# Attention norms of a hybrid decoder trunk: one product with ones from folded squares

## The chip, the core and the metric

The kernel runs on one core of a Trainium2 chip. The metric is device time in microseconds (us) of one launch. Its engines work side by side, each from its own queue in order: PE (TensorE, matrix products, with weight loads listed as PEld), DVE (VectorE), ACT (ScalarE), POOL (GpSimd) and SP (SyncE, which here only issues transfers). Engines wait for each other by semaphores. An instruction that waits holds up everything behind it in the same queue.

## The reference, cut to what matters

One decoder layer over 1024 positions and 1024 channels. The input is normalised, one wide product gives queries, keys, values and gates of two head groups, each group's output is normalised per head and gated, and a last product mixes them:

```python
h = rms_norm(x, pre_g)
z = jnp.einsum('bsd,de->bse', h, w_in)
qa, ka, va, ga, qb, kb, vb, gb, gk_low = split_columns(z)
...
oa = diff_attention(...)                                  # 8 heads, 128 value channels each
oa = rms_norm(oa, subln_g) * (1.0 - lam_init)             # mean square over the 128 channels of a head
oa = oa.reshape(B, S, DA_WIDTH) * jax.nn.silu(ga)
...
ob = rms_norm(gla_chunked(...), gla_g)                    # 4 heads, 256 channels each
y = jnp.einsum('bse,ed->bsd', jnp.concatenate([oa, ob], axis=-1), w_out)
return x + rms_norm(y, post_g)
```

The change is in the second line of the middle part: the mean square of each attention head over its 128 channels.

## The kernel before, in words

All products run on PE in a reduced-precision type (fp32r). To keep float32 accuracy an operand is split in two parts: ACT copies it to fp32r (the high part), DVE subtracts that copy from the original (the low part), and PE multiplies the parts one after the other into the same accumulator.

The kernel has three stages. Up to about 650 us it makes the wide input product and, woven into it, the gated linear attention. From there to about 965 us it runs the softmax attention together with a large part of the output product. Then it ends with the last quarter of the output product and the last norm.

In the attention stage `merge` weaves three streams together by a cost that each step yields: `all_scores` (line 1065; scores, mask and minimum on DVE, exponential on ACT, combination of the two maps on POOL and DVE at lines 1053 and 1056), `all_values` (line 1171; transposes of the weights on PE, their split into `wt_hi` on ACT at line 1096 and `wt_lo` on DVE at line 1097, products `po` with the values) and `out_early` (line 1238; products `ypart`, later `yps`, of the output product). The position of every PE instruction is fixed by this weave (`mm` and `tr`, lines 116 and 119, keep program order). The order on ACT, DVE and SP is not: there the library's scheduler places every instruction that isn't pinned, by a plan of its own made when the kernel is built. So an edit can change the order of instructions on ACT and DVE that it doesn't touch.

`attn_norm(h, half, o)` (line 1128) runs 16 times, for 8 heads and two halves of 512 positions. Its operand `o` holds one head's 128 value channels in 128 rows and 512 positions in columns. It works like this:

- ACT squares `o` into `sq` (line 1135), ACT makes the high part of `sq` in `hl[:, 0]` (line 1137), DVE the low part in `hl[:, 1]` (line 1138).
- After two steps of the weave that give other streams' work to PE, PE multiplies both parts with a 128 x 128 matrix of ones (`ms`, lines 1142 to 1144): the sum over the 128 rows, the same in every row.
- ACT makes the inverse root (lines 1148 and 1149), DVE scales `o` (line 1150), POOL multiplies by the gate (line 1151), SP stores the result to memory (`mixd`, line 1153). For the last head the result stays on chip, and `last_part` (line 1215) splits it for the output product: ACT makes `m_hi` at line 1218, DVE `m_lo` at line 1219.

`early_ends` (line 1324) is what PE does between the last head's two norms: it starts with the half that was normalised first, so PE's products `yps` there need `m_hi` and `m_lo` of that half while the other half's norm is being made.

Of the kernel before, what the change touches and what calls it, by code (L numbers as in the profile page):

```python
# [8 lines left out]
F32 = mybir.dt.float32  # L9
F32R = mybir.dt.float32r  # L10
AF = mybir.ActivationFunctionType
ALU = mybir.AluOpType
PSUM = bass.MemoryType.PSUM

P = 128
# [16 lines left out]
def hymba_kernel(  # L32
# [21 lines left out]
    act, dve, pool, pe, sp = nc.scalar, nc.vector, nc.gpsimd, nc.tensor, nc.sync  # L54

    def fp(t):
        return t.bitcast(F32)

    def cols(half):
        return slice(half * 512, half * 512 + 512)  # L60
# [8 lines left out]
    ones = const.tile([P, P], F32R, name="ones")  # L69
# [34 lines left out]
    def bank(i, shape, name):  # L104
        return psum.tile(shape, F32, tag=f"b{i}", name=name)
# [10 lines left out]
    def mm(*a, **k):  # L116
        tc.keep_in_program_order(pe.matmul(*a, **k))  # L117
# [99 lines left out]
    i = order.index((1, 4))  # L217
# [520 lines left out]
    decay(3)  # L738


    def mean_square(os, tile):

        sq = tile("sq")
        act.activation(sq, os[0], AF.Square)
        for o in os[1:]:
            sq2 = tile("sq")
            act.activation(sq2, o, AF.Square)
            dve.tensor_tensor(sq, sq, sq2, ALU.add)
        return sq
# [18 lines left out]
    def gla(g):  # L768

        u = None  # L770
        for half in range(2):
# [46 lines left out]
            for m in range(2):  # L818
# [14 lines left out]
                yield  # L833
            gla_loads(*((g, 1) if half == 0 else (g + 1, 0)))
            sq = mean_square([o[:, 0], o[:, 1]], t_c)
            hl = kp.tile([P, 2, 512], F32R, tag="k1", name="sq_hl")
            act.copy(hl[:, 0], sq)
# [133 lines left out]
    smp = smp_cm.__enter__()  # L971
# [156 lines left out]
    def attn_norm(h, half, o):  # L1128
        if h < DA_HEADS - 1:
            gate = smp.tile([P, 512], F32, tag="gate", name="gate", bufs=2)  # L1130
        else:
            gate = kp.tile([P, 512], F32, tag=("q1", "k1")[half], name="gate")
        sp.dma_start(gate, g_d[h][:, cols(half)])
        sq = smp.tile([P, 512], F32, tag="r", name="sq", bufs=1)
        act.activation(sq, o, AF.Square)
        hl = smp.tile([P, 2, 512], F32R, tag="sq_hl", name="sq_hl", bufs=1)
        act.copy(hl[:, 0], sq)
        dve.tensor_tensor(hl[:, 1], sq, fp(hl[:, 0]), ALU.subtract)
        yield 0.0
        yield 0.0  # L1140
        n_tr[0] += 1
        ms = bank(TR[n_tr[0] % 2], [P, 512], "ms")
        for i in range(2):
            mm(ms, ones, hl[:, i], start=(i == 0), stop=(i == 1))
        if h == DA_HEADS - 1 and not half:
            opened[TR[n_tr[0] % 2]] = None
        r = smp.tile([P, 512], F32, tag="r", name="r", bufs=1)
        act.activation(r, ms, AF.Ln, bias=eps_t, scale=1.0 / P)
        act.activation(r, r, AF.Exp, scale=-0.5)
        dve.scalar_tensor_tensor(r, o, sub_g, r, ALU.mult, ALU.mult)  # L1150
        pool.tensor_tensor(gate, r, gate, ALU.mult)
        if h < DA_HEADS - 1:
            sp.dma_start(mixd[h * P : (h + 1) * P, cols(half)], gate)
            stored.append(h)
        else:
            last_mix[half] = gate
        yield 0.0
# [13 lines left out]
    def all_values():  # L1171
        carry = iter(())
        nxt = v_first
        for h in range(DA_HEADS):
            v = nxt
            o = [smp.tile([P, 512], F32, tag="o", name="o", bufs=3) for _ in range(2)]
            yield from mingle(values(h, 3, v, o[1]), carry)
            if h + 1 < DA_HEADS:
                nxt = load_v(h + 1)
            yield from values(h, 2, v, o[1])  # L1180
            yield from mingle(
                chain(values(h, 1, v, o[0]), values(h, 0, v, o[0])), attn_norm(h, 1, o[1])
            )
            carry = attn_norm(h, 0, o[0])
        yield next(carry)
        yield lambda: (ENDS[2], 0) in ps_d
        early_ends()
        yield from carry
# [313 lines left out]
```

## Time and profile before

| | |
|---|---|
| median of 3 runs | 1001.05 us (999.26 to 1002.24) |
| the profiled execution's own time | 1001.76 us |
| its span, first to last instruction | 1000.1 us |
| `ms` products | 32, first at 685.3 us, last at 961.3 us |
| `attn_norm` calls | 16 |

The profile gives for each engine its busy time, for groups of instructions their mean time and what ended the idle time ahead of them, and a chain of waits followed back from the last instruction. Times in it are microseconds from the span's start unless marked ns. In a timeline row the first number is the start, the second the duration, and a remark in brackets is idle time of that engine just before, with what ended it. A row of matmuls with "x2" merges two. A PE duration runs from the start to the modelled end of a pipelined product, so the distance between two starts, not the duration, says what a product costs PE.

### The profile page before, as it was taken

The numbers are of one execution on the slowest core, as the hardware profiler recorded it, in microseconds if no ns is written. First come the engines' busy times: TensorE is split into PE (matmuls) and PEld (weight loads), VectorE is DVE, ScalarE is ACT, GpSimd is POOL, SyncE is SP. The second block draws the span as 40 slices with busy tenths as digits, with TensorE's granted clock in tenths as the row PEclk, the third lists the DMA queues.
The fourth block names the chain that finished last, engine by engine and source line by source line (L and its number), as shares of the span: only waits on it lengthen the run. The fifth ranks groups of instructions, "written<-read, shape, count | busy, mean of one in ns | idle before, by whom it ended". The sixth has DMA issues, their size and how long they took to land.

```text
span 1000.1 us, 16216 instructions
## 1 busy us (share of the span) xinstructions
PE 971.5 (97%) x5546; PEld 845.6 (85%) x5546; DVE 726.2 (73%) x1434; ACT 595.5 (60%) x1164; POOL 135.6 (14%) x145
## 2 busy tenths in 40 slices
PE   6999999999999999999999999999999999999997
PEld 5998988888889997998888888788888888888775
DVE  6886697789767487566777675577777787877646
ACT  7642464586465455445557665367666667777764
POOL 5200000000000000000200000022221232343232
PEclk9999999999999999999999999999999999999999
DMA  9443366746766678886978867996565679974658
GB/s 354 130 120 101 112 165 213 236 154 230 257 222 191 212 242 259 262 248 212 288 230 270 263 211 260 317 349 198 182 222 192 198 273 365 293 187 80 171 178 171
DMA packets 152595, 220.48 MB, mean 220 GB/s; under 512 B 17104, under 2 KB 83664, under 8 KB 152416
## 3 DMA queue, kind: packets, MB, share of 16 engines
q1 hardware_dynamic: 148480, 212.10, 65.3%
q0 software_dynamic: 4032, 7.34, 4.8%
q8 instruction: 44, 0.72, 0.3%
q14 instruction: 39, 0.32, 0.1%
HBM read 133.93 MB, written 88.60 MB: 223 GB/s over the span
## 4 chain that ended last, share of the span: by engine, by line
PE 83%; DMA 5%; DVE 4%; ACT 3%; issue 2%; POOL 1%; SPq 0%; DVEq 0%; POOLq 0%; ACTq 0%
PE x L117 21%; PE y L117 14%; PE z L117 14%; PE ypart L117 11%; PE sc L117 6%; PE po L117 4%; PE yps L117 3%; PE gpo L117 2%; PE wtr L120 2%; DMA v_d<-v_st 1%; PE kv L117 1%; DMA wo_raw<-in_w_out_dram 1%; DVE p L1037 1%; PE gkl_ps L117 1%; POOL p L1053 1%
## 5 line engine op out<-in xcount | busy, mean ns | idle before, releaser
L315 ACT CAST w<-w_raw 128x512 fp32r<-128x512 f32 (+1 forms) x164 | 112.7, 688 | 95.0 <-PE y L117 48.5
L316 DVE TENSOR_TENSOR w<-w_raw,w 128x512 fp32r<-128x512 f32 (+1 forms) x164 | 127.0, 776 | 56.3 <-ACT w L315 46.8
L1047 ACT ACTIVATE p<-p,stt 128x896 f32<-128x896 f32 (+7 forms) x128 | 99.5, 778 | 46.7 <-DVE stt L1037 45.5
L428 ACT COPY s<-x 128x512 f32<-128x512 f32 x84 | 49.0, 583 | 102.0 <-PE x L117 101.8
L1037 DVE CUSTOM_DVE_ANT_0 p<-sc,maskt 128x512 f32<-128x512 f32 (+3 forms) x128 | 74.8, 586 | 26.1 <-PE sc L117 25.0
L1053 POOL TENSOR_SCALAR p<-p,stt,lam 128x1024 f32<-128x1024 f32 (+3 forms) x64 | 54.9, 863 | 252.6 <-DVE stt L1052 252.3
L296 DVE TENSOR_TENSOR w_raw<-w_raw 128x512 f32<-128x512 f32 (+1 forms) x96 | 75.4, 786 | 16.2 <-DMA w_raw<-in_w_in_dram 15.0
L117 PE MATMUL y<-h_hi,w 128*128 128x512 f32 x320 | 81.2, 396 | 0.0
L117 PE MATMUL z<-s_hi,w 128*128 128x512 f32 x320 | 80.2, 393 | 0.0
L785 POOL TENSOR_SCALAR_AFFINE_SELECT gan<-gan 128x512 f32<-128x512 f32 x8 | 13.0, 1631 | 494.0 <-ACT gan L784 494.0
L117 PE MATMUL x<-s_hi,w 128*128 128x512 f32 x320 | 80.0, 392 | 0.0
L117 PE MATMUL ypart<-wo_hi,m_hi 128*128 128x512 f32 x192 | 79.5, 414 | 0.1
L117 PE MATMUL ypart<-wo_hi,m_lo 128*128 128x512 f32 x192 | 75.6, 394 | 0.0
L117 PE MATMUL ypart<-wo_lo,m_hi 128*128 128x512 f32 x192 | 75.4, 393 | 0.0
L117 PE MATMUL sc<-k,q 128*128 128x512 f32 (+1 forms) x192 | 70.7, 371 | 2.1 <-DVE stt L1037 2.1
L117 PEld LDWEIGHTS y<-h_hi,w 128*128 128x128 f32 x320 | 60.2, 191 | 12.1
L117 PEld LDWEIGHTS x<-s_hi,w 128*128 128x128 f32 x320 | 59.4, 188 | 11.9
L117 PEld LDWEIGHTS z<-s_hi,w 128*128 128x128 f32 x320 | 59.2, 188 | 11.7
L117 PE MATMUL sc<-ks,q 128*128 128x512 f32 (+1 forms) x192 | 66.6, 349 | 0.0
L1056 DVE SCALAR_TENSOR_TENSOR p<-p,stt,p 128x1024 f32<-128x1024 f32 (+3 forms) x64 | 52.6, 824 | 15.1 <-POOL p L1053 14.5
L117 PEld LDWEIGHTS po<-wt_hi,v 128*128 128x128 f32 x320 | 54.1, 188 | 7.1 <-ACT wt_hi L1096 0.8
L117 PE MATMUL po<-wt_hi,v 128*128 128x256 f32 (+1 forms) x320 | 58.9, 275 | 0.6 <-ACT wt_hi L1096 0.6
(220 smaller groups left out, 2273.6 us busy)
## 6 DMA issues: line engine op xcount, KB each, us to landing
w_raw<-in_w_in_dram SPq DMA_DIRECT2D x56, 512.0 KB, 4.6
wo_raw<-in_w_out_dram SPq DMA_DIRECT2D x32, 256.0 KB, 3.4
k_d<-qk_st SPq DMA_DIRECT2D x64, 128.0 KB, 2.5
q_d<-qk_st SPq DMA_DIRECT2D x64, 128.0 KB, 3.6
wo_d<-wo_hi SPq DMA_DIRECT2D x32, 256.0 KB, 2.6
wo_d<-wo_raw SPq DMA_DIRECT2D x32, 256.0 KB, 3.2
v_d<-v_st SPq DMA_DIRECT2D x64, 128.0 KB, 3.6
q<-q_d SPq DMA_DIRECT2D x32, 256.0 KB, 5.4
```

The lines of the kernel that those rows point to most:

```text
L117: tc.keep_in_program_order(pe.matmul(*a, **k))
L120: tc.keep_in_program_order(pe.transpose(dst, src, ident))
L296: dve.tensor_tensor(dst, a, b, ALU.subtract)
L315: act.copy(w[0], src)
L316: dve.tensor_tensor(w[1], src, fp(w[0]), ALU.subtract)
L428: act.copy(b[k], ps)
L785: pool.affine_select(a, a, [[0, 4], [1, P]], ALU.is_ge, 0.0, base=0, channel_multiplier=-1)
L1037: ins = dve.tensor_tensor_reduce(p[:, a:e], sc[:, : e - a], maskt[:, NZ + P - (e - a) :] if last else maskt[:, : e - a], 1.0, 3e38 if i == ...
L1047: act.activation(p[:, :n], p[:, :n], AF.Exp, bias=st[:, m : m + 1], scale=-1.0, accum_out=st[:, 2 + m : 3 + m],)
L1053: pool.tensor_scalar(p1[:, :n], p1[:, :n], st[:, 5:6], lam, ALU.mult, ALU.mult)
L1056: dve.scalar_tensor_tensor(p0[:, :n], p0[:, :n], st[:, 4:5], p1[:, :n], ALU.mult, ALU.subtract)
```

## The change

```diff
+    def both_parts(dst, src):
+
+        act.copy(dst[:64], src[:64])
+        dve.tensor_tensor(dst[64:], src[:64], fp(dst[:64]), ALU.subtract)
...
         sq = smp.tile([P, 512], F32, tag="r", name="sq", bufs=1)
-        act.activation(sq, o, AF.Square)
         hl = smp.tile([P, 2, 512], F32R, tag="sq_hl", name="sq_hl", bufs=1)
-        act.copy(hl[:, 0], sq)
-        dve.tensor_tensor(hl[:, 1], sq, fp(hl[:, 0]), ALU.subtract)
+        fold = smp.tile([P, 512], F32, tag="fold", name="fold", bufs=1)
+        act.activation(fold[:64], o[64:], AF.Square)
+        act.activation(sq[:64], o[:64], AF.Square)
+        dve.tensor_tensor(sq[:64], sq[:64], fold[:64], ALU.add)
+        both_parts(hl[:, 0], sq)
         yield 0.0
         yield 0.0
         n_tr[0] += 1
         ms = bank(TR[n_tr[0] % 2], [P, 512], "ms")
-        for i in range(2):
-            mm(ms, ones, hl[:, i], start=(i == 0), stop=(i == 1))
+        mm(ms, ones, hl[:, 0], start=True, stop=True)
```

Rows 64 to 127 of `o` are squared into rows 0 to 63 of a new tile, rows 0 to 63 into `sq`, and DVE adds the two. The sum has 64 rows. Its high part goes to rows 0 to 63 of `hl[:, 0]`, its low part to rows 64 to 127, so that one product with ones sums both. A norm then has two squares and a copy on ACT (before: one and a copy), an addition and a subtraction on DVE (before: a subtraction), all on 64 rows of 512, and one product on PE (before: two). The new tile takes 2 KB a row of its own; no other tile gets another place.

On PE the two programs have the same order but for the 16 products that are gone. On DVE and ACT the scheduler also places other instructions differently around the norms. The DVE orders at the places that the text below speaks of, with `p 512` for the minimum of line 1037 at 512 columns, `recip` for line 1052 and `p896` for line 1056 at 896 columns:

```
first norm of the first head:
  before  recip, p 512, p896, p 256, r, p 512, wt_lo
  after   p 512, recip, p 256, p896, r, p 512, wt_lo
  (the fifth head's first norm had this second order before, too)
second norm of the third head:
  before  p 512, wt_lo, p768, sq_hl, p 128, wt_lo, p 512
  after   p 512, sq, p768, wt_lo, p 128, wt_lo, sq_hl
second norm of the fourth head:
  before  wt_lo, p 512, p768, sq_hl, p 128, wt_lo, p 512
  after   p 512, sq, p768, wt_lo, p 128, wt_lo, sq_hl
second norm of the seventh head:
  before  p 512, p768, wt_lo, sq_hl, p 128, m_lo, wt_lo, m_lo
  after   p 512, sq, p768, wt_lo, p 128, m_lo, wt_lo, sq_hl, m_lo
last norm of all:
  before  sq_hl, m_lo x4
  after   sq, sq_hl, m_lo x4
```

On SP a store or a load of two heads stands one to three transfers earlier or later; POOL's order is the same.

## The prediction

> **What bounds the kernel now.** I read the page first: busy time, granted clock and the engines' shares of the chain of waits.
>
> ```profile
> PE 971.5 (97%) x5546; PEld 845.6 (85%) x5546; DVE 726.2 (73%) x1434; ACT 595.5 (60%) x1164; POOL 135.6 (14%) x145
> PEclk9999999999999999999999999999999999999999
> PE 83%; DMA 5%; DVE 4%; ACT 3%; issue 2%; POOL 1%; SPq 0%; DVEq 0%; POOLq 0%; ACTq 0%
> ```
>
> PE is busy almost throughout at its full granted clock, and 83% of the chain is PE's own work. A pipelined engine can look busier than it is, so the second view is the busy time by stretch: attention up to where its last norms begin, and the 25 us that hold those two.
>
> ```profile
> 665.00:940.00 275.00, 273.57 (x1592) 237.30 (x1591) 209.72 (x576) 195.28 (x436) 81.81 (x89) 1.00 0.72 220
> 940.00:965.00 25.00, 23.19 (x119) 18.23 (x118) 7.22 (x18) 12.85 (x30) 1.94 (x3) 1.00 0.47 159
> ```
>
> The columns are PE, PEld, DVE, ACT and POOL. Up to 940 us PE has no idle time to speak of (1.4 of 275 us), but DVE is at 76% and ACT at 71%; after that PE has gaps. So the first stretch is PE's with two engines close behind, and the second is a chain between PE, ACT and DVE. The third view is what PE's weight loads wait for in the attention stage, longest first:
>
> ```profile
> PEld po L117 <- DVE wt_lo L1097: 3.1, 9, 0.9
> ```
>
> Nine times PE already stands still because DVE's low part of the transposed weights (`wt_lo`) comes too late. DVE's reserve there is a matter of tenths of a microsecond, and the change puts work on DVE.
>
> **What is removed.** 16 products with ones go. What one costs PE is the distance between starts, not its duration of 394 ns:
>
> ```profile
> 685.33 0.62 PE L117 MATMUL ms<-sq_hl,ones 128*128 128x512 f32 x2
> 685.79 0.39 PE L117 MATMUL po<-wt_hi,v 128*128 128x256 f32 x2
> ```
>
> Two take 0.46 us (685.33 to 685.79), so one takes 0.23 us. The last norm of all gives nothing: behind its products PE waits for `m_hi` of the other half, which ACT makes behind a copy that has nothing to do with this norm:
>
> ```profile
> 961.57 0.39 PE L117 MATMUL yps<-wo_hi,ones 128*128 128x512 f32 x1
> 962.18 0.50 PE L117 MATMUL yps<-wo_hi,m_hi 128*128 128x512 f32 x1 [0.22 <-ACT m_hi L1218]
> ```
>
> The product behind `ms` starts at 961.57 and is issued by 961.80; the next one starts at 962.18, so 0.38 us are lost there already, and 0.23 us more or less ahead of them change nothing. That leaves 15 x 0.23 = 3.5 us saved.
>
> **What is added.** ACT gets one more square, DVE one more addition per norm, all on 64 rows. The trace has no 64-row instruction, but it has both ends:
>
> ```profile
> L1135 ACT ACTIVATE sq<-o x16: 631/633/634, 678.8 to 955.9; 128x512 f32<-128x512 f32 x16
> L1138 DVE TENSOR_TENSOR sq_hl<-sq,sq_hl x16: 680/688/694, 681.3 to 957.3; 128x512 fp32r<-128x512 f32 x16
> L748 DVE TENSOR_TENSOR sq<-sq x8: 684/690/693, 300.8 to 569.6; 128x512 f32<-128x512 f32 x8
> L676 DVE TENSOR_TENSOR gkl<-low,gkl x2: 680/680/681, 84.0 to 90.6; 16x512 fp32r<-16x512 f32 x2
> ```
>
> The same subtraction takes 680 ns on 16 rows, the addition 690 ns on 128: the number of rows doesn't matter, so 64 rows are as dear as 128. I take 0.63 us for the square and 0.69 us for the addition. Back to back they cost their queues about 0.53 and 0.61 us (below, 770.63 to 771.24 for a DVE instruction of this size). The way from `o` to the product grows by both: 0.64 + 0.02 + 0.69 + 0.02 = 1.37 us. For most norms two steps of the weave lie in between and cover it: the first norm's low part starts at 681.3 and is ready at 682.0, 3.3 us ahead of its product at 685.33. The copy on ACT now waits for DVE's addition, where before it followed ACT's own square; behind it stand `wt_hi` and exponentials, for which `wt_lo`, `po` and the scores' combination wait. In most norms the scheduler has put the copy one to three instructions further back, so that the addition is done by then. The delay shows where DVE's queue had no reserve, or where nothing lies in between. I went through the places where the two programs' DVE orders differ.
>
> *The last norm of all* (second half of the last head). This piece of the chain of waits is made of the norm's own steps:
>
> ```profile
> 955.95 0.64 ACT sq L1135
> 956.61 0.63 ACT sq_hl L1137
> 957.26 0.22 DVE sq_hl L1138
> 957.87 0.30 DVE m_lo L1219
> 958.22 3.07 PE yps L117 x12
> ```
>
> PE's `yps` products wait for `m_lo` of the other half. `m_lo` and the `m_hi` that it needs stand behind this norm's subtraction on DVE and its copy on ACT, and keep that place. Both start 1.37 us later, `m_lo` too, and PE has nothing else in front: +1.4 us, not covered.
>
> *The first head's first norm.* The combination `p896` now stands behind the next scores' `p 256`, and `recip`, which feeds POOL's half of it, behind `p 512`. The trace has a case of that order, at the fifth head:
>
> ```profile
> 840.17 0.48 DVE L1037 CUSTOM_DVE_ANT_0 p<-sc,maskt,stt 128x256 f32<-128x256 f32 x1 [1.30 <-PE sc L117]
> 840.58 1.15 DVE L1056 SCALAR_TENSOR_TENSOR p<-p,stt,p 128x896 f32<-128x896 f32 x1
> 842.38 0.40 PE L117 MATMUL po<-wt_hi,v 128*128 128x256 f32 x2
> 843.52 0.39 PE L117 MATMUL po<-wt_lo,v 128*128 128x256 f32 x1 [0.75 <-DVE wt_lo L1097]
> ```
>
> DVE stands idle until the scores come, everything behind is late, and PE loses 1.14 - 0.24 = 0.9 us (0.24 is the undisturbed distance, 771.87 to 772.11 below). At the first head the old order kept `wt_lo` ready 0.15 us ahead of its use:
>
> ```profile
> 689.36 0.56 DVE L1097 TENSOR_TENSOR wt_lo<-wtr,wt_hi 128x384 fp32r<-128x384 f32 x1
> 690.07 0.29 PE L117 MATMUL po<-wt_lo,v 128*128 128x256 f32 x1
> ```
>
> With the fifth head's order: +0.9 us.
>
> *Second norms of the third, fourth and seventh heads.* There `wt_lo` moves behind the addition and, in the first two, behind `p768` (0.92 us from start to start):
>
> ```profile
> 770.63 0.69 DVE L1097 TENSOR_TENSOR wt_lo<-wtr,wt_hi 128x512 fp32r<-128x512 f32 x1
> 771.24 1.01 DVE L1056 SCALAR_TENSOR_TENSOR p<-p,stt,p 128x768 f32<-128x768 f32 x1
> 772.16 0.68 DVE L1138 TENSOR_TENSOR sq_hl<-sq,sq_hl 128x512 fp32r<-128x512 f32 x1
> 771.87 0.40 PE L117 MATMUL po<-wt_hi,v 128*128 128x256 f32 x2
> 772.11 0.28 PE L117 MATMUL po<-wt_lo,v 128*128 128x256 f32 x1
> ...
> 808.05 0.69 DVE L1097 TENSOR_TENSOR wt_lo<-wtr,wt_hi 128x512 fp32r<-128x512 f32 x1
> 810.25 0.28 PE L117 MATMUL po<-wt_lo,v 128*128 128x256 f32 x1
> ...
> 925.38 0.68 DVE L1097 TENSOR_TENSOR wt_lo<-wtr,wt_hi 128x512 fp32r<-128x512 f32 x1
> 926.12 0.38 PE L117 MATMUL po<-wt_lo,v 128*128 128x256 f32 x1
> ```
>
> Third head: 0.61 + 0.92 = 1.53 us later against a reserve of 772.11 - 771.32 = 0.79: +0.7. Fourth: `p 512` comes in front too, 0.61 + 0.61 + 0.92 = 2.14 against 1.51: +0.6. Seventh: only the addition, 0.61 against nothing (0.06): +0.6.
>
> *The product itself.* At the seventh head the subtraction moves behind the second `wt_lo`:
>
> ```profile
> 927.83 0.69 DVE L1097 TENSOR_TENSOR wt_lo<-wtr,wt_hi 128x512 fp32r<-128x512 f32 x1
> 927.84 0.63 PE L117 MATMUL ms<-sq_hl,ones 128*128 128x512 f32 x2
> 928.58 0.33 PE L120 MATMUL wtr<-ident,p 128*128 128x128 f32 x1
> ```
>
> It would end at 927.83 + 0.61 + 0.69 = 929.1, 1.3 us after the product's turn. Of that 0.6 is the stall just counted and 0.3 the gap in which PE stood behind the product anyway (928.58, not 928.30): +0.4.
>
> *All other places.* 14 norms put 14 x 0.61 = 8.5 us more on DVE in the first stretch, whose idle time falls from 65.3 to 56.8 us. If waits go as busy over idle, 209.7/65.3 becomes 218.2/56.8, and the 3.1 us of waits for `wt_lo` grow by a fifth: +0.7 us. Its bounds are 0 and, with every one of 14 norms late by the full 1.37 us less what is named, some 16 us; the row of 3.1 us is the nearest, so I stay by it.
>
> ACT's square lies inside its 29% idle time where it isn't counted above; without that cover it would be 14 x 0.53 = 7.4 us. The new tile has a place of its own and moves no other. The few transfers that change places on SP move by one to three issues; SP's queue has 0% of the chain (SPq above), so I count nothing, and the worst of it lies inside the bound just given. POOL's queue keeps its order.
>
> [...]
>
> **Sum.** -3.5 + 1.4 + 0.9 + 0.7 + 0.6 + 0.6 + 0.4 + 0.7 = +1.8 us. The profiled execution took 1001.76 us (span 1000.1 plus 1.7 around it): 1003.6 us. The median of the three runs is 0.7 lower, so against that the forecast is +0.25%. What a measurement of this kernel can tell from no change is 0.3%, 3.0 us around 1001.05: 998.05 to 1004.05.
>
> **Rivals.**
>
> *The reserve suffices.* The 16 products go and only the chain at the very end pays: -3.5 + 1.4 = -2.1, 999.7 us, or 998.3 if that is covered as well; less the 0.7, 997.6 to 999.0 as medians. For it: PE takes its products in a fixed order, and the first norm leaves its product 3.3 us of reserve. Against: the row of nine waits for `wt_lo`.
>
> *DVE becomes the bound* (the other side). If the reordered queue leaves DVE late at half of the 14 norms by the 0.9 us of the fifth head, beyond what is named, that is 7 x 0.9 = 6.3 instead of 0.7: 1003.6 + 5.6 = 1009.2 us. It decides from where DVE's idle time in the stretch (57 us) no longer falls ahead of `wt_lo` but between scores, as at 840.17, which shows 1.30 us of it.
>
> *Saved and paid back.* The scheduler's order differs from what runs; if the first head's case and two of the `wt_lo` cases don't come true, 2.2 us less is paid: -0.4, 1001.4 us.
>
> **How the numbers follow.** Forecast 0.60, its own range +0.5 to +5 us as unnamed waits are more likely missed than invented: about half of it over 1004.05. Reserve suffices 0.14, two thirds of it under 998.05. DVE as the bound 0.16. Paid back 0.10, within. Faster 0.10; slower 0.31 + 0.16 = 0.47; same the rest, 0.43. The range leaves out the lower part of the second case and the upper part of the third: 998.5 to 1008.5.
>
> **What would show it.** `ms` products: 16, each 0.23 us from its neighbour. Squares 0.63 us and additions 0.69 us on 64 rows; another number there moves every term. At the end, about 1.4 us more between `o` and the `yps` product that waits for `m_lo`. A wait of `po` for `wt_lo` of 0.6 to 0.9 us at the four named heads; the total of PE's waits for `wt_lo` near 7 us instead of 3.1. Wrong it would be if PE waits for `ms` at many norms, if ACT is what `po` waits for, or if the time differs outside 665 to 965 us.

## The result, and the profile after

| | before | after |
|---|---|---|
| median on one chip, 22 runs each | 1001.15 us (997.44 to 1005.37) | 1005.97 us (1001.01 to 1078.86) |
| ratio | | 1.0044, 95% interval 1.0031 to 1.0056 |
| span of the profiled execution | 1000.1 us | 1004.5 us |
| `ms` products | 32 | 16 |

The one run of 1078.86 us had a granted clock of 0.851, against 0.992 to 0.999 in the others, and is left out of the ratio. The change makes the kernel 4.4 us slower (3.1 to 5.6). The sign is the forecast's and the time lies inside its range; its sum of +1.8 us is 2.6 too small. In the profile of after line numbers behind the new function are 5 or 6 higher (`wt_lo` is now line 1102, the copy 743, the subtraction 744).

The page of after, the same three lines as before: busy times, granted clock in 40 slices, shares of the chain of waits.

```profile
PE 969.3 (96%) x5530; PEld 842.6 (84%) x5530; DVE 736.8 (73%) x1450; ACT 602.8 (60%) x1180; POOL 141.6 (14%) x145
PEclk9999999999999999999999999999999999999999
PE 77%; DMA 9%; DVE 5%; ACT 3%; issue 2%; SPq 1%; POOL 1%; DVEq 0%; ACTq 0%; POOLq 0%
```

PE has 16 instructions fewer, and its share of the chain falls from 83% to 77%. DMA rises from 5% to 9%. The chain is one path among several that end nearly together, so these shares are no amounts of lost time; PE's idle time says more. Busy time by stretch (PE, PEld, DVE, ACT, POOL, granted clock):

```profile
665.00:940.00 275.00, 269.30 (x1566) 232.90 (x1565) 216.30 (x581) 198.35 (x442) 82.95 (x88) 1.00 0.71 220
940.00:965.00 25.00, 20.88 (x113) 16.70 (x112) 9.54 (x23) 13.37 (x30) 2.27 (x3) 1.00 0.56 155
```

In the first stretch PE's idle time went from 1.4 to 5.7 us, in the second from 1.8 to 4.1. Until 665 us the two traces don't differ in kind: the first `ms` starts at 685.3 us in both. What PE's weight loads wait for between 665 and 965 us:

```profile
PEld po L117 <- DVE wt_lo L1102: 7.0, 13, 1.0
PEld yps L117 <- ACT yps L1360: 2.3, 1, 2.3
```

There are thirteen waits for `wt_lo` instead of nine, 7.0 us instead of 3.1. So what was taken from PE came back as waits. The groups of the norm's own instructions (min, median, max in ns, first and last start):

```profile
L1142 ACT ACTIVATE fold<-o x16: 629/631/632, 678.8 to 958.9; 64x512 f32<-64x512 f32 x16
L1144 DVE TENSOR_TENSOR sq<-sq,fold x16: 676/678/685, 681.3 to 960.2; 64x512 f32<-64x512 f32 x16
L744 DVE TENSOR_TENSOR sq_hl<-sq,sq_hl x16: 684/685/690, 683.2 to 961.6; 64x512 fp32r<-64x512 f32 x16
L117 PE MATMUL ms<-sq_hl,ones x16: 389/393/497, 685.3 to 965.5; 128*128 128x512 f32 x16
```

Half the rows take the same time: 631 ns for a square of 64 rows against 633 on 128, 685 against 688 for the subtraction. PE's timeline at five heads (start, duration, and in brackets the idle time ahead with its cause):

```profile
690.75 0.38 PE L117 MATMUL po<-wt_lo,v 128*128 128x256 f32 x1 [0.73 <-DVE wt_lo L1102]
...
772.37 0.39 PE L117 MATMUL po<-wt_lo,v 128*128 128x256 f32 x1 [0.62 <-DVE wt_lo L1102]
...
811.24 0.39 PE L117 MATMUL po<-wt_lo,v 128*128 128x256 f32 x1 [0.61 <-DVE wt_lo L1102]
...
889.68 0.39 PE L117 MATMUL po<-wt_lo,v 128*128 128x256 f32 x1 [0.61 <-DVE wt_lo L1102]
...
928.17 0.39 PE L117 MATMUL po<-wt_lo,v 128*128 128x256 f32 x1 [0.63 <-DVE wt_lo L1102]
```

These are the first head's first norm and the second norms of the third, fourth, sixth and seventh heads. The prediction named four of them; the sixth it did not. There, too, the addition stands right ahead of `wt_lo` on DVE:

```profile
888.35 0.68 DVE L1144 TENSOR_TENSOR sq<-sq,fold 64x512 f32<-64x512 f32 x1
888.95 0.68 DVE L1102 TENSOR_TENSOR wt_lo<-wtr,wt_hi 128x512 fp32r<-128x512 f32 x1
```

The seventh head's second norm: two pieces of the chain of waits, then DVE and PE:

```profile
924.51 4.12 DMA m_raw<-mixd
...
928.65 0.52 ACT m_hi L1326
```

```profile
929.20 0.56 DVE L1327 TENSOR_TENSOR m_lo<-m_raw,m_hi 128x384 fp32r<-128x384 f32 x1 [0.82 <-ACT m_hi L1326]
929.69 0.69 DVE L1102 TENSOR_TENSOR wt_lo<-wtr,wt_hi 128x512 fp32r<-128x512 f32 x1
930.41 0.69 DVE L744 TENSOR_TENSOR sq_hl<-sq,sq_hl 64x512 fp32r<-64x512 f32 x1
931.12 0.56 DVE L1327 TENSOR_TENSOR m_lo<-m_raw,m_hi 128x384 fp32r<-128x384 f32 x1
931.15 0.50 PE L117 MATMUL ms<-sq_hl,ones 128*128 128x512 f32 x1 [1.09 <-DVE sq_hl L744]
```

The subtraction now stands behind `m_lo` and `wt_lo`; `m_lo` itself waits for a transfer through ACT's `m_hi`, and the `ms` product for all of it. Then a transfer (SP's queue, PE, and the same piece in the chain of waits; last, PE in before):

```profile
936.97 0.32 SPq L1159 DMA_DIRECT2D mixd<-gate  x1
937.47 8.39 SPq L1307 DMA_DIRECT2D yp<-y_d  x4
```

```profile
942.40 0.51 PE L117 MATMUL yps<-wo_hi,m_hi 128*128 128x512 f32 x1 [1.86 <-ACT yps L1360]
```

```profile
937.47 4.27 DMA yp<-y_d
941.74 0.02 issue
941.76 0.60 ACT yps L1360
```

```profile
937.94 0.50 PE L117 MATMUL yps<-wo_hi,m_hi 128*128 128x512 f32 x1 [0.25 <-ACT yps L1354]
...
941.94 0.50 PE L117 MATMUL yps<-wo_hi,m_hi 128*128 128x512 f32 x1 [0.50 <-ACT yps L1354]
```

The product before that `yps` starts at 940.14, so PE loses 942.40 - 940.14 - 0.23 = 2.0 us there. In before the same way cost two waits, from start to start 0.42 and 0.66 us. The last norm in the chain of waits (gaps of 0.02 to 0.04 us, listed as `issue`, are left out):

```profile
958.90 0.63 ACT fold L1142
959.55 0.64 ACT sq L1143
960.22 0.70 DVE sq L1144
960.93 0.63 ACT sq_hl L743
961.58 0.69 DVE sq_hl L744
962.30 0.30 DVE m_lo L1225
962.65 3.07 PE yps L117 x12
```

From `o` to `m_lo` there are five steps where there were three.

### The profile page after: what moved, and what is told of

The parts are those of the page before. It is cut to its first block, busy times and chain, and to the rows that moved or that the text cites. A ratio compares the mean times of both kernels' runs of the same rounds, so it can differ in the third digit from the quotient of the medians.

```text
span 1004.5 us, 16197 instructions
## 1 busy us (share of the span) xinstructions
PE 969.3 (96%) x5530; PEld 842.6 (84%) x5530; DVE 736.8 (73%) x1450; ACT 602.8 (60%) x1180; POOL 141.6 (14%) x145
## 4 chain that ended last, share of the span: by engine, by line
PE 77%; DMA 9%; DVE 5%; ACT 3%; issue 2%; SPq 1%; POOL 1%; DVEq 0%; ACTq 0%; POOLq 0%
PE x L117 21%; PE y L117 14%; PE z L117 14%; PE ypart L117 8%; PE sc L117 4%; PE yps L117 4%; PE po L117 4%; PE gpo L117 2%; DMA ks<-k_d 2%; PE wtr L120 2%; DMA mixd<-gate 2%; DVE p L1042 1%; PE kv L117 1%; DVE p L1061 1%; DMA v_d<-v_st 1%
## 5 line engine op out<-in xcount | busy, mean ns | idle before, releaser
L790 POOL TENSOR_SCALAR_AFFINE_SELECT gan<-gan 128x512 f32<-128x512 f32 x8 | 17.3, 2166 | 492.3 <-ACT gan L789 492.3
```

Of the source, the lines that this page charges most:

```text
L790: pool.affine_select(a, a, [[0, 4], [1, P]], ALU.is_ge, 0.0, base=0, channel_multiplier=-1)
```

## The experiments

One measure is used throughout. A is the time from the first `ms` product to that of the 14th norm (the seventh head's second), B from there to the 16th, each from the starts in one profiled execution (before: 685.33, 927.84 and 961.11). The ratio is that of the timed runs (4 to 12 of each kernel, 21 of the change) to those of before on the same chip. A and B are of a single execution each. Up to the 14th norm the change, "last norm the old way" and "loads of `yp` ahead" are the same program, and their A is 245.8, 245.5 and 246.4 us: a difference of A under 1 us alone says nothing.

| kernel | A, us | B, us | ratio, 95% interval |
|---|---|---|---|
| before | 242.5 | 33.3 | |
| one product, old order | 239.9 | 33.1 | 0.9988 (0.9978 to 0.9998) |
| new order only | 244.6 | 33.5 | 1.0031 (1.0017 to 1.0045) |
| new order, extra square | 244.8 | 34.2 | 1.0025 (1.0008 to 1.0043) |
| new order, extra addition | 247.1 | 33.4 | 1.0046 (1.0028 to 1.0064) |
| new order, both | 247.7 | 34.1 | 1.0050 (1.0036 to 1.0064) |
| the change, product made twice | 248.1 | 35.8 | 1.0084 (1.0066 to 1.0102) |
| the change (after) | 245.8 | 34.4 | 1.0044 (1.0031 to 1.0056) |
| last norm the old way | 245.5 | 34.6 | 1.0032 (1.0017 to 1.0047) |
| loads of `yp` ahead | 246.4 | 35.0 | 1.0053 (1.0036 to 1.0069) |
| the change in the old order | 259.5 | 37.3 | 1.0208 (1.0191 to 1.0225) |
| addition on GpSimd | 243.9 | 37.1 | 1.0040 (1.0026 to 1.0054) |
| that, last norm the old way | 243.9 | 34.6 | 1.0021 (1.0002 to 1.0039) |
| high part only | 238.2 | 33.7 | 0.9947 (0.9934 to 0.9961) |

To hold an order, a helper adds edges between neighbours on one engine, which bind the scheduler and make nothing wait (shortened):

```diff
+    def keep_order(engine, places):          # traced: the engine's instructions in program order
+        for a, b in zip(places, places[1:]):
+            tc.add_manual_dep(traced[b], traced[a].name, NoSync, reason="keep_order")
```

### One product alone, and three steps from before to after

The first kernel:

```diff
-        for i in range(2):
-            mm(ms, ones, hl[:, i], start=(i == 0), stop=(i == 1))
+        mm(ms, ones, hl[:, 0], start=True, stop=True)
+    keep_order("DVE", ...)    # ACT and POOL too: the order of before
```

> The kernel before with one product of ones per norm (the product of the low part is left out, so the sums lack it; the low part is still made), VectorE, ScalarE and GpSimd held to the issue order of before. Theory (PE bounds, and 15 of 16 products are worth 0.23 us each): 3.5 us faster than before, ratio 0.9965. Rival (the products lay in waits that PE had anyway): within 0.5 us of before.

A falls by 2.6 us for 13 products (13 x 0.23 = 3.0), so PE is the bound there. In the timed runs only 1.2 us arrive (0.2 to 2.2), under the 3.5 expected. One place where it goes is seen on PE:

```profile
936.98 0.50 PE L117 MATMUL yps<-wo_hi,m_hi 128*128 128x512 f32 x1 [1.57 <-ACT yps L1353]
```

PE comes 2 us earlier to the products that need `yp`, and the transfer doesn't: the waits grow from 0.42 + 0.66 to one of 1.74 us. What takes the rest in the timed runs stays open.

The second kernel is before with nothing but the order of after:

```diff
+    keep_order("DVE", ...)    # ACT, POOL and SP too: the order of after, fold and addition taken out
```

> The kernel before, same instructions and same two products, but VectorE, ScalarE, GpSimd and SyncE held to the issue order of the changed kernel (its squares of 64 rows and additions taken out of the list). Theory (of the 7.9 us that the change costs beside its saving, the fuller VectorE and the longer chain of the norm make most): 0.5 to 3 us slower than before, about +2. Rival 1 (the scheduler's new order is the cost): 6 to 8 us slower. Rival 2 (the order costs nothing): within 0.5 us.

3.1 us slower (1.7 to 4.5), A 2.1 us longer: the order costs something by itself, but not all. PE's waits for `wt_lo` between 665 and 945 us are 2.4 us in before, and with the new order:

```profile
PEld po L117 <- DVE wt_lo L1097: 3.8, 10, 0.9
```

The third adds the load, into a tile that nothing reads:

```diff
         hl = smp.tile([P, 2, 512], F32R, tag="sq_hl", name="sq_hl", bufs=1)
+        fold = smp.tile([P, 512], F32, tag="fold", name="fold", bufs=1)
+        act.activation(fold[:64], o[64:], AF.Square)
         act.activation(sq, o, AF.Square)
+        dve.tensor_tensor(fold[:64], fold[:64], o[:64], ALU.add)
         act.copy(hl[:, 0], sq)
```

> As the run with the order alone, and each norm also makes the square of the upper 64 rows on ScalarE and an addition of 64 rows on VectorE at the changed kernel's places, but into a tile that nothing reads: the load without the longer chain, still two products. Theory (VectorE's added 16 x 0.68 us is the largest cost): 2 to 4 us slower than the run with the order alone, about 5 us slower than before. Rival (it is the chain, since copy and subtraction wait for the addition): within 1 us of the run with the order alone.

A grows by another 3.1 us, B by 0.6, as the theory has it; by the ratios it is 1.9 us, just under the expected 2 to 4, and the intervals overlap. The fourth is the changed kernel with the saving given back:

```diff
-        mm(ms, ones, hl[:, 0], start=True, stop=True)
+        for i in range(2):
+            mm(ms, ones, hl[:, 0], start=True, stop=True)
```

> The changed kernel with its product of ones made twice (the second overwrites the first with the same values), held to its own issue order: order, load and chain, without the saving. Theory (PE still sets the pace after the change, so the saving is real): 3.5 us slower than the changed kernel, 7 to 8.5 us slower than before; and the step from the run with order and load, 2 to 3 us, is the chain. Rival (PE's waits now swallow the saved product): within 1 us of the changed kernel, 4 to 5.5 us slower than before.

8.4 us slower than before (6.6 to 10.2), 4.0 slower than the changed kernel by the two ratios: the saving is real. In A, 13 products are worth 2.3 us, a little less than 3.0. For the longer chain the ratios give 3.4 us over the run with order and load, and the intervals don't touch. Of this A shows only 0.4 us. B is 1.7 us longer, but PE ran at half its clock for some 3.4 us of it in this execution (granted clock 0.83 over 960 to 970 us, last section), which makes up to 1.6 us, an estimate. The last norm (below) has 1.2 to 1.5 us of the chain's price; where the rest lies in the timed runs stays open.

### Which half of the load

```diff
+        act.activation(fold[:64], o[64:], AF.Square)              # this one alone,
+        dve.tensor_tensor(fold[:64], o[:64], o[:64], ALU.add)     # and in another kernel this one
```

> As the run with order and load (before's instructions and two products, the changed kernel's issue order), but of the load only ScalarE's square of the upper 64 rows into a tile that nothing reads; the additions are left out. Between the first and the last product of ones the order alone took 2.3 us over before, order and load 6.0. Theory (VectorE, the fuller engine, makes the load's 3.7 us): at most 1 us over the run with the order alone. Rival (ScalarE's 16 x 0.63 us, ahead of copies that the scores wait for, makes it): 2.5 to 3.7 us over it.

> The other half of that load: only VectorE's addition of 64 rows into a tile that nothing reads, the extra square left out. Theory (VectorE makes the load's 3.7 us): 2.5 to 3.7 us over the run with the order alone, first product of ones to last. Rival (ScalarE): at most 1 us over it. If both halves give about 2 us each, neither engine is the one.

Over the run with the order alone, A grows by 0.2 us with the square and by 2.5 us with the addition. In B it is the other way round: the square costs 0.8 us, the addition nothing. PE's waits for `wt_lo` between 665 and 945 us, with the square alone and, below it, with the addition alone:

```profile
PEld po L117 <- DVE wt_lo L1097: 3.8, 10, 1.0
```

```profile
PEld po L117 <- DVE wt_lo L1097: 6.7, 12, 1.0
```

The square changes nothing against the order alone; the addition makes 3.8 us into 6.7, which is also the sum of the changed kernel in that window (6.7, 12 waits). The run with both gives 6.6. So VectorE's theory holds for A: 14 additions bring 2.5 us of waiting. The ratios order the two the same way, though their intervals overlap.

### The last norm

```diff
+        folded = h < DA_HEADS - 1 or half          # the last norm: as before
+        if folded:
             fold = smp.tile([P, 512], F32, tag="fold", name="fold", bufs=1)
...
+        else:
+            act.activation(sq, o, AF.Square)
+            act.copy(hl[:, 0], sq)
+            dve.tensor_tensor(hl[:, 1], sq, fp(hl[:, 0]), ALU.subtract)
```

> The changed kernel in its own issue order, with the last of the 16 norms made in the old way (one square of 128 rows, copy, subtraction, two products). Theory (that norm's longer chain stands in the chain of waits before the last products, priced +1.4 in the prediction): 1.2 to 1.8 us faster than the changed kernel. Rival (other waits end there as late, the first block's m_hi among them): within 0.5 us of it.

From the 15th norm's product to the 16th's it takes 9.56 us, in the changed kernel 11.02: 1.46 us less, as expected. By the ratios 1.2 us arrive (the intervals overlap). In the profiled execution B is not shorter, since PE ran at half its clock for 3.4 us at another place:

```profile
942.65 0.50 PE L117 MATMUL yps<-wo_hi,m_hi 128*128 128x512 f32 x1 [1.98 <-ACT yps L1370]
...
944.41 0.63 PE L117 MATMUL yps<-wo_hi,m_lo 128*128 128x512 f32 x1
944.84 0.63 PE L117 MATMUL yps<-wo_lo,m_hi 128*128 128x512 f32 x1
```

```profile
945.00:950.00 5.00, 5.00 (x27) 4.29 (x26) 1.41 (x3) 2.41 (x5) 0.00 (x0) 0.78 0.45 145
```

Products that start 0.23 us apart elsewhere start 0.43 apart here. The window shows a granted clock of 0.78, the 5 us ahead of it 0.88: at 0.50 that is 3.4 us. The wait of 2.1 us for `yp` stands just ahead.

### The loads of `yp`

```diff
     keep_order("SP", ...)
-    mixd store, yp, yp, yp, yp
+    yp, yp, yp, yp, mixd store
```

> The changed kernel in its own issue order, but on SyncE's queue the store of the seventh head's second norm result stands behind the four loads of yp that it stood ahead of. Theory (the loads of yp stand behind that store, which waits for GpSimd's gate, and PE's wait of 2.0 us at 940 us comes from there): that wait falls under 0.7 us, 1.0 to 1.8 us faster in all. Rival (the loads wait for their buffers, which the stores of y_d free as late): within 0.5 us.

The theory falls. What SP waits for between 915 and 950 us:

```profile
SPq L1307 <- DMA y_d<-yst: 11.1, 2, 9.2
```

With the store out of the way the first load still starts at 936.96 us (937.47 in the changed kernel), since its buffer is freed by an earlier transfer out of it (`y_d` from `yst`). PE's waits there are 0.54 and 0.94 us in this execution, but the seventh head's `ms` waits 1.86 instead of 1.25, and nothing is gained: 5.3 us slower than before (3.6 to 6.9).

### Is the new order a fault?

```diff
+    keep_order("ACT", ...)    # the order of before (POOL and SP too); fold right ahead of sq
+    keep_order("DVE", ...)    # the order of before; the addition right ahead of the subtraction
```

> The changed kernel held to the issue order of before on VectorE, ScalarE, GpSimd and SyncE: each extra square right before the old one, each addition right before its subtraction, which stays in its old place. Theory (the new order is the scheduler's answer to the longer chain; in the old one the copy and the subtraction wait in their queues with others' work behind them): over 8 us slower than before. Rival (the order was a choice that cost 2.3 us for nothing): that 2.3 us come back, some 2 us slower than before.

20.8 us slower than before (19.1 to 22.5). What ACT waits for between 665 and 970 us, and PE's loads up to 965:

```profile
ACT sq_hl L743 <- DVE sq L1144: 25.5, 15, 2.9
```

```profile
PEld po L117 <- DVE wt_lo L1102: 12.6, 15, 1.4
```

In the old place the copy waits for DVE's addition in 15 of 16 norms, up to 2.9 us, with exponentials and `wt_hi` behind it; in the changed kernel it waits 2.0 us in four. The new order costs 2.1 us in A by itself; the old one with the change in it costs 17.0. So the new order is no fault but the cheaper of the two.

### Addition elsewhere, and what would be faster

```diff
-        dve.tensor_tensor(sq[:64], sq[:64], fold[:64], ALU.add)
+        pool.tensor_tensor(sq[:64], sq[:64], fold[:64], ALU.add)
```

> The changed kernel with the addition of the two halves on GpSimd, the scheduler's own order. VectorE loses 16 x 0.68 us; GpSimd's product of 128x512 takes 1.29 to 1.87 us, so the norm's chain is 0.6 us or more longer. Theory (of the load it is VectorE's part that PE waits for, 2.4 us alone): 2 to 4 us faster than the changed kernel, within 2 us of before. Rival (the length of the chain decides): within 1 us of the changed kernel, or slower.

In all it is no different from the changed kernel (1.0040 against 1.0044), as the rival says, but two opposite effects show. A falls by 1.9 us, as it should without VectorE's additions; but the scheduler's order differs, too (PE's stall at the first head falls from 0.89 to 0.20 us), and the two weren't tried apart. B grows by 2.7: from the 15th to the 16th norm it takes 0.7 us longer, the wait for `yp` is 2.5 us, 0.5 longer, and behind it the halved clock (0.88 from 935 to 940 us, 0.78 from 940 to 945) costs 1.3. And GpSimd's addition is not free for VectorE here (timeline of both):

```profile
921.50 1.28 POOL L1144 TENSOR_TENSOR sq<-sq,fold 64x512 f32<-64x512 f32 x1
...
922.03 1.58 DVE L1061 SCALAR_TENSOR_TENSOR p<-p,stt,p 128x768 f32<-128x768 f32 x1
```

A combination of 768 columns takes 1.01 us in before and in the changed kernel, 1.58 here, started while GpSimd adds. The longest combination of any size takes 1.92 us here, 1.29 in the changed kernel.

> As the run with the addition on GpSimd, and the last norm in the old way. Theory: 1 to 2 us faster than that run, since the last norm's chain is not hidden; then at or a little under the time of before (1 us slower to 2 us faster). Rival: no difference from that run beyond 0.5 us.

2.1 us slower than before (0.2 to 3.9), 1.9 less than without the old last norm. It is the best version of the change tried here that keeps both parts, and it doesn't beat the kernel before.

The last kernel drops what stands around the product as well as the second product:

```diff
-        sq = smp.tile([P, 512], F32, tag="r", name="sq", bufs=1)
-        act.activation(sq, o, AF.Square)
-        hl = smp.tile([P, 2, 512], F32R, tag="sq_hl", name="sq_hl", bufs=1)
-        act.copy(hl[:, 0], sq)
-        dve.tensor_tensor(hl[:, 1], sq, fp(hl[:, 0]), ALU.subtract)
+        hl = smp.tile([P, 512], F32R, tag="sq_hl", name="sq_hl", bufs=1)
+        act.activation(hl, o, AF.Square)
...
-        for i in range(2):
-            mm(ms, ones, hl[:, i], start=(i == 0), stop=(i == 1))
+        mm(ms, ones, hl, start=True, stop=True)
```

> The kernel before with ScalarE's square written straight as the high part and one product; the low part is left out (no copy, no subtraction), so the sums lack it, as in the run with one product. Theory (VectorE's and ScalarE's work around the norms is what PE waits for, beside the products): 3 to 5 us faster than before, and 1 to 3 us faster than the run that left out the product alone. Rival (only PE's product counts): the same as that run, 1 to 2 us faster than before.

5.3 us faster than before (3.9 to 6.6), and the only kernel here that is clearly faster. Busy time up to 940 us and PE's waits up to 965:

```profile
665.00:940.00 275.00, 271.71 (x1588) 236.10 (x1588) 203.41 (x562) 189.65 (x423) 81.78 (x89) 1.00 0.73 222
```

```profile
PEld yps L117 <- ACT yps L1350: 3.7, 3, 2.5
PEld po L117 <- DVE wt_lo L1097: 1.4, 5, 0.4
```

Waits for `wt_lo` fall from 3.1 to 1.4 us, although the products went as well. The waits for `yp` (3.7 us) take a part of it. The two kernels with half the products differ by 4.1 us by the ratios and by 1.7 in A (this one in the scheduler's own order, which wasn't tried apart). By the ratios leaving out copies and subtractions as well gained more than leaving out the products alone did (1.2 us); by A it gained less (2.6). That it gained something both say.

## Why the prediction was right or wrong

*What bounds.* Right. PE is the bound in the attention stage, and DVE the engine close behind: the products given back cost 4.0 us, the additions alone 2.5 us in A.

*The sums.* By its own rule the term for all other places is a fifth of 3.1 us, 0.6 and not 0.7. And +1.8 us is 0.18% of the time; the +0.25% sets a sum that stands on one execution against a median 0.7 us lower, which is no part of the change.

*The saving, -3.5.* Right for the changed kernel (4.0 by the ratios with wide intervals, 2.3 of 3.0 in A). In before's surroundings the same saving was worth 1.2 by the ratios, 2.6 in A.

*The durations on 64 rows.* Right: 631 ns and 678 ns against 630 and 690.

*The last norm, +1.4.* Right: 1.46 back with the old way (1.2 by the ratios, not clear of noise); its product gains nothing, as said.

*First, third, fourth and seventh head, +0.9, +0.7, +0.6, +0.6.* The places and sizes are right: the pairs ahead start at 689.63, 771.35, 810.22 and 927.13, so from start to start, less the undisturbed 0.24, PE loses 0.89, 0.78, 0.78 and 0.80 us (0.18 of the last stood there before). The first comes with the order alone. At the other three PE loses 0.18 to 0.22 us with the order alone and 0.78 to 0.79 with the addition: it is the addition ahead of `wt_lo`, as argued. The total of waits for `wt_lo` was put near 7 and is 7.0 us, though in part from a place that wasn't named (below).

*`ms` at the seventh head, +0.4.* Too small in this execution. PE loses 1.25 us ahead of the product, where before lost 0.29 behind it: about +1.0, 0.6 more than the term. The step took `m_lo` and the second `wt_lo` at before's times. But `m_lo` waits for `m_hi` and that for a transfer, so the subtraction, now behind it, inherits the transfer's lateness (0.82 us of idle time ahead of `m_lo`; 0.42 in before). Three other profiles with this order show the size change with it: 0.78, 0.79 and 1.86 us.

*All other places, +0.7.* This is where most of the missing 2.6 us lies. Found in the trace: 0.77 at the sixth head's second norm, 0.5 where transposes behind the fifth head's second `ms` wait for `wt_lo`, and 0.95 more at `yp` (2.03 against 0.42 + 0.66). That is 2.2 instead of 0.7; with the 0.6 above, 2.1 of the 2.6 us. An estimate by busy over idle can't see any of it: two are single places without reserve, and the third is not DVE's at all. The sixth head belonged in the named list: with the order alone PE loses 0.16 us there, with the addition 0.77, as at the third and fourth, so the walk through the places where DVE's order differs left one out.

*SP counted as nothing.* Wrong as a reason: 0% of the chain in before did not mean that transfers had slack. The chain there already ran through them, and DMA's 5% became 9%. Which transfer sets `yp` was not what I supposed after the result either: the first load comes 0.5 us earlier without the store on SP ahead of it, and then waits for the stores that free its buffers.

*Rivals.* "The reserve suffices" and "saved and paid back" fall with the ratio's lower bound of 1.0031. "DVE becomes the bound" had the right kind of waits, but at five places with 0.6 to 0.9 us, not at half of 14.

*Gaps beside the subtraction.* At the seventh head `wt_lo` ends at 929.69 + 0.69 = 930.38 and the subtraction into rows 64 to 127 starts at 930.41, the next one at 931.12 behind 931.10; in before such neighbours overlap by 0.08 (771.24 against 770.63 + 0.69). In 15 of the 16 norms of after nothing overlaps the subtraction at its start (gaps of 0.02 to 0.08 us), and in all 16 nothing at its end (0.02 to 0.03, once 0.30 with a wait for `m_hi`); in the last norm it waits for the copy at its start. So each side loses about 0.11 us, 0.22 per norm and up to 3.5 us of DVE time in 16 norms, an estimate from these rows. The sum has no term for it. What sets the gaps these runs don't show. What they cost in time was not tried apart; in A it lies, with the rest of the longer chain, in the 0.4 us between the run with order and load and the run with the product made twice.

## What to carry to other kernels

A saved PE slot is worth its full price only as long as the engines that feed PE have reserve at each place where the queue changes: look for the places where an operand is ready with less reserve than the added instruction takes, one by one, and don't spread the rest by a mean (the additions alone brought 2.5 us of waiting in A here). A transfer that lands just in time keeps its time when PE comes earlier, so part of a saving can stop there, as with one product alone (1.74 us of waits instead of 0.42 + 0.66). If rows are folded to halve a product, the elementwise work isn't halved with them (here 631 ns for a square of 64 rows, 633 of 128). Look first for work that can be dropped on the bound engine and on the one that feeds it together: only that was clearly faster here.

## What the runs showed of the hardware

In some profiles PE runs at half its clock (0.50) for 3.4 us soon after a wait. In the run with the last norm the old way five steps between products of 512 columns are 0.43 us instead of 0.23 (944.41 to 946.55, above), behind a wait of 1.98 us that ends at 942.65. In the run with GpSimd's addition three are, behind a wait of 2.34 us that ends at 938.79. The granted clock by window shows such a stretch in the attention stage of five kernels:

| kernel | window, us | granted clock |
|---|---|---|
| last norm the old way | 940 to 945, 945 to 950 | 0.88, 0.78 |
| the change, product made twice | 960 to 965, 965 to 970 | 0.83, 0.83 |
| addition on GpSimd | 935 to 940, 940 to 945 | 0.88, 0.78 |
| that, last norm the old way | 935 to 940, 940 to 945 | 0.80, 0.86 |
| the change in the old order | 815 to 825 | 0.83 |

At 0.50 that is 3.4 us each time. Such a stretch holds some eight products at 0.43 us, each 0.20 us late: up to 1.6 us, an estimate from these rows. Waits of PE of 1.57 us (one product alone, at 936.98) and 1.86 us (the changed kernel, at 942.40) passed with a granted clock of 1.00 around them. Ahead of the attention stage before and after have such a stretch, too: the clock is 0.50 from 401.5 to 404.5 us in both and 1.00 up to 401, behind waits of 3.07 and 2.37 us that end at 400.74 and 400.09. Waits of 1.69 and 1.65 us at 467 us and of 1.23 us at 652 passed at 1.00 in both. Whether the wait brings the stretch about, and from what length on, these runs don't show.

Between 665 and 965 us the changed kernel has three waits over 1 us (1.09, 1.86 and 1.23) where before has none. The two profiled executions differ by the full 4.4 us with one such stretch each, at the same place, beside one in the last microseconds of both, so none of that difference comes this way. In the timed runs the mean granted clock is 0.9961 for the changed kernel and 0.9967 to 0.9970 for before (of before, only the runs on the experiments' three chips have it on record). Within the changed kernel's runs 0.001 of clock goes with 1.0 us. From these two figures some 0.6 to 0.9 of the 4.4 us come this way, an estimate. With GpSimd's addition the clock is 0.9954 and 0.9953.

In the run with GpSimd's addition, GpSimd's and DVE's instructions both take longer in places. The combination of 768 columns that starts at 922.03, while GpSimd adds, takes 1.58 us instead of 1.01, and the longest combination 1.92 instead of 1.29. The additions on GpSimd take 1.26 to 1.92 us, at a median of 1.29 and a mean of 1.48. The combinations' median stays at 0.75 us, as in the changed kernel. What makes some of them longer was not tried apart.
